# Weaving the last third of a linear attention with the first output tiles, and pairing half-array products, in a one-layer hybrid decoder

## The chip, the cores and the metric

The kernel runs on one core of one Trainium2 chip. Its time is the device time of one execution in microseconds (us). Three runs of the kernel before gave 1269.86, 1271.31 and 1274.69 us, so the median is 1271.31 us. One further execution was profiled; all rows below are from it.

A core has five engines with instruction queues of their own: PE (matrix products; a stationary matrix is loaded first, the loads are counted as PEld), DVE and ACT (vector work), POOL (slower vector work), and SP, which here issues all transfers between the main memory and the core's own memory. Each engine runs its instructions in the order in which they stand in its queue.

## What is computed

One inference step of a single decoder layer for a prompt of 2048 positions and for 8 samples of 8 new positions each (64 rows, called "the sample"; its attention reads a cache of 2048 positions per sample):

```python
h = rmsnorm(x, norm_w)
z = h @ w_in                      # 1024 -> 3600 columns
q, k, v, qb, kb, vb, g_lr, gate_a, gate_b = split(z)
o_a = dilated_attention(rope(rmsnorm(q)), rope(rmsnorm(k)), v)   # (128,1), (512,4), (2048,16)
log_a = log_sigmoid(g_lr @ w_gate_up + b_gate) / 16
o_b, state = gated_linear_attention(qb, kb, vb, log_a, s0)       # exact, in chunks
mixed = concat(o_a * silu(gate_a), rmsnorm(o_b) * silu(gate_b))
y = x + mixed @ w_out
```

The outputs are y for the prompt and the sample, the new keys and values, and the final states of the linear attention.

## The kernel before

**Precision.** The large products run in half precision with each factor split in a high and a low part. A prompt tile of 128 rows needs high·high, high·low and low·high: for each of the 8 slices of 128 along the inner dimension, three products of 128x512 columns, 24 in all (line 1742 for the input projection, line 2088 for the output). For the sample, high and low parts of its 64 rows stand side by side as the 128 columns of one stationary matrix (`hs`, `mh_s`), so that a product with the high weights gives both, and a second product with the low weights gives high·low and, unasked, low·low. That is 16 products for each block of columns (`sample_sum`, line 1434, and `finish` with n = 64). Afterwards the two halves of the 128 result rows are added.

**Stages.** The first stage projects q, k and v tile by tile and runs the first two dilations of the attention behind them (tiles `s`, `p`, `pt`, `t`, `O`). The second projects `qkb`, then `g` and `vb`, with the third dilation beside it. The linear attention of the prompt (`gla_prompt`, eight pieces e0 to e7 of 256 rows, that is 16 chunks; `gla_core` holds seven levels per piece, products `sc_e` at lines 853 and 869; the chunk's state update `U` at line 1900 and output `O` at lines 1908 and 1914) runs beside `g`, `vb` and `gb`. Then the scaled output weights `w_o0` and `w_o1` are made (`load_w`: a maximum over the weights through two small PE products `mx_o`, then eight steps on ACT, line 1272, and on DVE, line 1273). The last stage makes 16 output tiles (`prompt_out`): `combine` joins the three attention branches and the linear attention's output (`oc`, `mix`), `turned` transposes (`tm`, line 2052), `finish` multiplies (`Y`, two column blocks of 24 products) and adds x (`xr`, line 2095). The attention of the sample over its cache (`sample_pair`, products `OS` at line 2344 over value blocks `sv_b` of 1 MB, loaded at line 2375) runs beside it.

**What sets the order.** Two things. The Python code is written as generators, and `weave` takes the next step of the generator with the smallest share done, where each generator has a number of steps written beside it; this sets the order in which buffers of a pool are handed on. From that, `Plan` reads the instructions' dependences, forms priorities, changes some of them by a table of triples (`steps`) and lays down a fixed order for each engine. The table names instructions by number, so any change in the code asks for another table.

**Pools.** In the kernel before, `gla_all` (the linear attention) belongs to the `until` list of the weave with `gb` and the output weights, so in the code it is complete before `prompt_out` begins. The memory of the linear attention's pools (`c_gla`) is then released, and the sample attention's pools (`sk2` with six buffers of 1 MB for `sv_b`, and `ss1`) take its place: the first `sv_b` load cannot start before the last chunk has been stored.

## Time and profile before

| what | value |
|---|---|
| median of 3 runs | 1271.31 us |
| profiled execution | 1268.54 us |
| its span, first to last instruction | 1266.8 us |
| mean granted PE clock | 0.994 |
| PE busy | 1200.7 us, 95% |
| DVE busy | 956.7 us, 76% |
| ACT busy | 816.5 us, 64% |
| POOL busy | 553.5 us, 44% |
| mean rate of the transfers | 223 GB/s |

Times in the rows are counted from the span's first instruction. A row of groups or of the timeline names the line of the kernel, the engine, the operation, output<-inputs (buffer numbers left out), partitions x elements, the count, and in brackets how long the engine stood idle before it and what it waited for. A PE product takes longer from its start to its end than the distance at which products follow each other, so the cost of one is read from start to start. A product of 32-bit factors is two PE instructions in the profile.

### The profile page before, as it was taken

To read this page: it belongs to the slowest core of one execution; us is meant where nothing else is said; L and a number is where in the kernel's file an instruction comes from. 1 tells how busy PE (TensorE), PEld (TensorE's weight loads), DVE (VectorE), ACT (ScalarE), POOL (GpSimd) and SP (SyncE) were. 2 spreads that over 40 slices of the span, in tenths; PEclk is the share of its full clock that TensorE was granted. 3 is DMA by queue.
4 is the path that set the end of the run, shared out by engine and by line. 5 is a ranking of instruction groups with operands and counts; after the bars stand their busy time and mean duration, and the time that the engine had idled before them with its cause. 6 is when DMAs were issued, how large, how long until landed. Compare 5 with 4: busy or idle time off the path is not lost. (4 is left out here: it accounts for less than half of the span.)

```text
span 1266.8 us, 26198 instructions
## 1 busy us (share of the span) xinstructions
PE 1200.7 (95%) x8942; PEld 725.5 (57%) x8942; DVE 956.7 (76%) x2450; ACT 816.5 (64%) x2191; POOL 553.5 (44%) x475
## 2 busy tenths in 40 slices
PE   4999999999999899998999999999999979999998
PEld 2444465666567566766676756656555544545443
DVE  7887787899978867768777764798999793657652
ACT  6654597889589877968677642778779751322230
POOL 0154543666646334542443676655553341323310
PEclk9999999999999999999999999999999999999999
DMA  8579935876866798799999877675647279979941
GB/s 292 183 201 251 258 122 137 227 217 191 205 163 162 202 257 268 229 253 248 253 247 239 252 216 203 175 230 141 236 159 247 80 226 390 384 278 366 351 144 57
DMA packets 235831, 283.07 MB, mean 223 GB/s; under 512 B 116193, under 2 KB 146866, under 8 KB 232626
## 3 DMA queue, kind: packets, MB, share of 16 engines
q1 hardware_dynamic: 235698, 281.40, 74.7%
q8 instruction: 70, 1.15, 0.4%
q14 instruction: 63, 0.52, 0.1%
HBM read 183.02 MB, written 75.24 MB: 204 GB/s over the span
## 5 line engine op out<-in xcount | busy, mean ns | idle before, releaser
L1597 POOL TENSOR_TENSOR pr<-k,qb 128x512 f32<-128x512 f32 x128 | 167.0, 1304 | 178.4 <-DVE sck L1598 109.7
L1742 PEld LDWEIGHTS <-hr 128*128 128x128 f16 x1824 | 172.8, 98 | 114.1 <-issue 12.4
L1033 ACT ACTIVATE p<-p,o 128x256 f32<-128x256 f32 (+1 forms) x384 | 173.1, 456 | 31.5 <-DVE o L1030 29.0
L1742 PEld LDWEIGHTS <-hl 128*128 128x128 f16 x1248 | 119.9, 98 | 122.8 <-issue 10.3
L2088 PE MATMUL Y<-w_o,mh 128*128 128x512 f16 x768 | 178.8, 379 | 5.0 <-DVE w_o L1273 4.1
L1007 POOL TENSOR_TENSOR pt<-p,pt 128x512 f16<-128x512 f32 (+1 forms) x80 | 93.9, 1175 | 121.2 <-ACT pt L1006 112.9
L1055 PE MATMUL O<-v,pt 128*128 128x128 f16 x1200 | 131.4, 220 | 8.9 <-DVE pt L1003 2.5
L1040 PE MATMUL t<-ident,p 128*128 128x128 f32 x600 | 118.8, 279 | 3.3 <-DMA hr<-h_d 1.9
L2088 PEld LDWEIGHTS <-mh 128*128 128x128 f16 x768 | 72.1, 98 | 86.5 <-issue 12.2
L1598 DVE TENSOR_REDUCE sck<-pr 128x8 f32<-128x512 f32 x128 | 87.0, 680 | 43.6 <-POOL pr L1597 43.0
L1055 PEld LDWEIGHTS <-pt 128*128 128x128 f16 x1200 | 93.5, 98 | 39.0 <-POOL pt L1007 5.1
L1742 PE MATMUL acc_v<-w_v,hl 128*128 128x512 f16 x384 | 109.9, 381 | 0.1
L1742 PE MATMUL acc_q<-w_q,hl 128*128 128x512 f16 x384 | 106.4, 383 | 1.1 <-ACT zs_k L1317 0.8
L1742 PE MATMUL acc_k<-w_k,hl 128*128 128x512 f16 x384 | 104.1, 379 | 2.5 <-DVE vp L1404 2.5
L1742 PE MATMUL acc_g<-w_g,hr 128*128 128x272 f16 (+1 forms) x768 | 105.9, 278 | 0.0
L1742 PE MATMUL acc_vb<-w_vb,hr 128*128 128x512 f16 x384 | 97.6, 383 | 1.7 <-DVE so_g L1291 1.6
L1030 DVE CUSTOM_DVE_ANT_0 p<-s,m3w,scl_s 128x128 f32<-128x128 f32 (+1 forms) x256 | 87.8, 394 | 13.4 <-DMA o_d<-o 5.7
L1022 PE MATMUL s<-kk,qq 128*128 128x256 f16 (+1 forms) x512 | 88.2, 266 | 8.6 <-DMA kk<-kp_d 4.8
L1742 PE MATMUL acc_gb<-w_gb,hr 128*128 128x512 f16 x384 | 94.5, 380 | 0.1
L1040 PEld LDWEIGHTS t<-ident,p 128*128 128x128 f32 x600 | 75.0, 142 | 21.5 <-ACT p L1033 8.7
L2130 POOL TENSOR_TENSOR oc<-oc 128x512 f32<-128x512 f32 x32 | 42.4, 1343 | 100.8 <-DVE oc L2123 58.7
L1742 PE MATMUL acc_qkb<-w_qkb,hr 128*128 128x512 f16 x288 | 79.8, 379 | 0.0
(528 smaller groups left out, 2524.3 us busy)
## 6 DMA issues: line engine op xcount, KB each, us to landing
k<-in_cache_k_win SPq DMA_DIRECT2D x104, 256.0 KB
sv_b<-in_cache_v_win SPq DMA_DIRECT2D x24, 1024.0 KB
hr<-h_d SPq DMA_DIRECT2D x44, 512.0 KB
qb<-q_d SPq DMA_DIRECT2D x64, 256.0 KB
oc<-o_d SPq DMA_DIRECT2D x48, 264.0 KB
o_d<-o SPq DMA_DIRECT2D x64, 132.0 KB
x<-in_x_prompt SPq DMA_DIRECT2D x16, 512.0 KB
h_d<-hl SPq DMA_DIRECT2D x16, 512.0 KB
```

The lines of the kernel that those rows point to most:

```text
L1007: POOL.tensor_tensor(l, f, h, ALU.subtract)
L1022: PE.matmul(s_ps[:, i * w : (i + 1) * w], q, k, start=(n == 0), stop=(n == len(prods) - 1),)
L1030: DVE.tensor_tensor_reduce(s[:, sl], s_ps[:, sl], mask, neg, BIG, ALU.add, ALU.min, nmf(i))
L1033: ACT.activation(s[:, sl], s[:, sl], AF.Exp, bias=nmf(i), scale=-1.0, accum_out=denf(i))
L1040: PE.transpose(p_ps[:, i * P : (i + 1) * P], t["s"][:, i * P : (i + 1) * P], ident[:])
L1055: PE.matmul(o_, t["pt"][:, c, (i * nb + b) * P : (i * nb + b + 1) * P], vf(i, b), start=(n == 0), stop=(n == 2 * nb - 1),)
L1597: POOL.tensor_tensor(pr[:], kt, qt, ALU.mult)
L1598: DVE.tensor_reduce(out, pr[:].rearrange("p (u k d) -> p u k d", u=2, k=4), AX.X, ALU.add)
L1742: PE.matmul(z, a_[:, k, :], w[:, p_, k, cols], start=(k == 0 and i == 0), stop=(k == KT - 1 and i == 2),)
L2088: PE.matmul(Y[:], a_[:, k, :], w_[:, part, k, :512], start=(i == 0), stop=(i == len(prods) - 1),)
L2130: eng.tensor_tensor(o_[g], o_[g], w[:, g].unsqueeze(2).to_broadcast([P, NH, HD]), ALU.mult)
```

## The change

Four edits, and a new table.

1. **Half products.** A new function `sample_products` replaces the 16 full products of the sample. The 8 with high weights stay as they were. The 8 with low weights now use only the 64 columns of the high part as the stationary matrix, and put their 64 result rows in turn into the lower and the upper half of the accumulator; the sum of the two halves, which is taken afterwards anyway, holds all of them. The product low·low is no longer computed. This holds for the eight column blocks of the input projection (v, q, k, qkb, g0, g1, vb, gb) and the two of the output.
2. **Weave.** `gla_all` gets 60 instead of 155 steps in the first weave and 10 instead of 45 in the one with `gb`, which makes it take fewer turns there; it leaves the `until` list of that weave, and what is left of it is woven with `prompt_out` (60 steps). `combine(t+2)` waits until its chunk is done.
3. **Scales.** `inv_o0` and `inv_o1` (line 2217) are made before the output tiles begin, in another pool; the tile `bnd` is gone and `smx` serves in its place.
4. **Pools.** The small tiles `qs` and `qr` of the q and k projection move from pool `sm` to pool `xp`.
5. **Plan.** Another table of steps; 3 instead of 12 rounds of priorities, and 800 instead of 900 ns added to a transfer's landing.

```diff
-                ss = sm.tile([P, 2 * NH], F32, name=f"qs_{nm_}_{t}", tag="qs")
+                ss = xp.tile([P, 2 * NH], F32, name=f"qs_{nm_}_{t}", tag="qs", bufs=2)
...
+        def sample_products(out, hs, w, order):
+
+            for i, k in enumerate(order):
+                PE.matmul(out, hs[:, k, :], w(0, k), start=(i == 0), stop=False)
+            for i, k in enumerate(order):
+                r0 = NS * (i % 2)
+                PE.matmul(
+                    out[r0 : r0 + NS], hs[:, k, 0:NS], w(1, k), start=False, stop=(i >= KT - 2)
+                )
+
         def sample_sum(acc, w, hs, c0, ncol):
 
-            prods = [(part, k) for k in range(KT) for part in range(2)]
-            for i, (part, k) in enumerate(prods):
-                PE.matmul(
-                    acc[:, :ncol], hs[:, k, :], w[:, part, k, c0 : c0 + ncol],
-                    start=(i == 0), stop=(i == len(prods) - 1),
-                )
+            sample_products(
+                acc[:, :ncol], hs, lambda part, k: w[:, part, k, c0 : c0 + ncol], range(KT)
+            )
...
-        gla_all = [chain(sample_gla(), *(gla_prompt(e) for e in range(8))), 155]
+        gla_all = [chain(sample_gla(), *(gla_prompt(e) for e in range(8))), 60]
...
-        gla_all[1] = 45
+        gla_all[1] = 10
...
+                if n < P:
+                    sample_products(Y[:], mh, lambda part, k: w_[:, part, k, :512], ks)
+                for i, (k, a_, part) in enumerate(prods if n == P else ()):
...
                     if i == 1 and t + 2 < NT:
+                        while t + 2 not in mixed:
+                            yield WAIT
                         mixes[t + 2] = combine(t + 2)
...
-        weave(host, gla_all, fetch, mixed_first, until=[host, gla_all, fetch, mixed_first])
+        left = weave(host, gla_all, fetch, mixed_first, until=[host, fetch, mixed_first])
+        for nh in range(2):
+            DVE.tensor_scalar(
+                inv_o[nh][:], p2[:], loaded[f"o{nh}"][1][:], 1.0 / M_SCALE, ALU.mult, ALU.mult
+            )
+        out = [prompt_out(), 2 * NT * KT + 30]
+        if left:
+            gla_all = left[0]
+            gla_all[1] = 60
+            out = weave(gla_all, out, until=[gla_all])[0]
...
-        "1:9738:-1587 1:8521:-604 0:11378:-6896 2:12183:-36893 0:12042:-1940 0:7618:-507 "
+        "0:7339:-3039 0:9273:-5212 1:8590:-9900 0:9000:-2297 1:10685:2313 0:13065:3357 2:11182:-7159 "
...
-    plan.fix(plan.settle(12, 900.0, 1.15, 60.0, 10.0, steps))
+    plan.fix(plan.settle(3, 800.0, 1.15, 60.0, 10.0, steps))
```

Line numbers move: what stood at 1742 stands at 1749, 2088 at 2095, 2375 at 2383. The new half products are at line 1440, the full ones of the sample at 1437.

How the order moves, at three places. First PE where the sample's product of block `gb` stands. Before, its 16 full products (line 1438) stand there. Now, in the middle of its low-weight part (`hs` is the sample's stationary matrix, `hr_15` that of prompt tile 15, `sc_e0` a level of the linear attention's first piece, `O_s` the linear attention of the sample):

```order
L1749 MATMUL acc_vb_15_12620<-w_vb_8468,hr_15_11930 128x512
L1440 LDWEIGHTS hs_249
L1440 MATMUL acc_gb_s_12731<-w_gb_11380,hs_249 64x512
L869 MATMUL sc_e0_1_10056<-qbd0_9599,kq_e0_10021 64x64 x8
L1977 MATMUL O_s_9879<-vb_s_9873,Ac_smp_9675 64x128
L1749 LDWEIGHTS hr_15_11930
```

Here a half stands alone among other products; five of the eight halves of this block do. For the other nine blocks the two halves of a pair stand next to each other.

Second PE around the last chunk of the linear attention, `O_15`. Before, within the first output tile:

```order
L2052 MATMUL tm_1_1_14329<-ident16_83,mt_1_14077 128x128
L2088 LDWEIGHTS mh_0_14119
L2088 MATMUL Y_0_0_14217<-w_o0_13586,mh_0_14119 128x512
L1908 MATMUL O_15_13304<-Sbd1_9605,kq_e7_13053 128x256
L1914 MATMUL O_15_13304<-vb_15_13297,full_9609 128x128 x2
```

And now:

```order
L2095 MATMUL Y_4_1_14566<-w_o1_13492,mh_4_14424 128x512
L2095 LDWEIGHTS mh_5_14591
L2095 MATMUL Y_5_0_14642<-w_o0_13018,mh_5_14591 128x512
L1915 MATMUL O_15_14790<-Sbd1_9605,kq_e7_14281 128x256
L1921 MATMUL O_15_14790<-vb_15_14783,full_9609 128x128 x2
```

The last chunk moves from the first output tile to the sixth; chunks 8 to 15 now stand behind the last products of `gb`.

Third the queue of SP where the first value blocks of the sample are loaded. Before:

```order
L914 DMA ob_d_66<-ob_c15_13329 128x512
L2077 DMA xr_3_14675<-in_x_prompt 128x1024
L2105 DMA oc_4_14510<-o1_d_67 128x528
L2105 DMA oc_4_14510<-o2_d_68 128x528
L2105 DMA oc_4_14510<-o3_d_69 128x528
L2260 DMA Sc_0_14280<-sc_d_70 128x2x128
L2302 DMA sm_0_14475<-in_c_smask 128x448
L2304 DMA mc_0_14477<-in_c_smult 128x64
L2375 DMA sv_0_0_b2_14574<-in_cache_v_win 128x2048
```

And now:

```order
L2112 DMA oc_10_15218<-o3_d_69 128x528
L2118 DMA gal_10_15225<-ga_d_65 128x512
L2225 DMA out_state_gla_prompt<-Sbd0_9601 64x128
L2106 DMA out_y_prompt<-xr_4_14492 128x1024
L2118 DMA obl_11_15381<-ob_d_66 128x512
L2118 DMA gwl_11_15382<-gw_d_64 128x512
L914 DMA ob_d_66<-ob_c15_14815 128x512
L2085 DMA xr_8_15209<-in_x_prompt 128x1024
L2268 DMA Sc_0_14924<-sc_d_70 128x2x128
L2310 DMA sm_0_15069<-in_c_smask 128x448
L2383 DMA sv_0_0_b2_15128<-in_cache_v_win 128x2048
```

The first value block stood behind the operands of output tile 4 (`oc_4`); it now stands behind those of tile 10.

## The prediction

> **What bounds the kernel now.** I read the totals first, then PE by stage, then PE's waits in the worst stage.

> ```profile
> PE 1200.7 (95%) x8942; PEld 725.5 (57%) x8942; DVE 956.7 (76%) x2450; ACT 816.5 (64%) x2191; POOL 553.5 (44%) x475
> ```

> PE is busy for 1200.7 of 1266.8 us; 66.1 us are left in which it stands. The table by stage (length, then busy time of PE, PEld, DVE, ACT and POOL, PE's clock, the share and rate of the transfers) says where:

> ```profile
> 0.00:50.00 50.00, 33.07 (x189) 17.41 (x190) 38.14 (x100) 27.10 (x45) 0.85 (x7) 1.00 0.80 274
> 50.00:1000.00 950.00, 916.51 (x6900) 581.02 (x6899) 761.55 (x2007) 715.03 (x2020) 485.21 (x412) 0.99 0.76 209
> 1000.00:1050.00 50.00, 39.89 (x317) 23.71 (x316) 41.96 (x103) 25.57 (x55) 20.06 (x19) 1.00 0.62 206
> 1050.00:1250.00 200.00, 198.77 (x1485) 98.07 (x1484) 110.57 (x236) 48.75 (x73) 47.38 (x38) 1.00 0.79 297
> 1250.00:1266.80 16.80, 12.44 (x58) 5.31 (x56) 4.50 (x6) 0.00 (x0) 0.00 (x0) 0.99 0.15 47
> ```

> PE stands 16.9 us at the start, 33.5 us spread over 950 us, 10.1 us in the 50 us between the linear attention and the output tiles, 1.2 us in the output stage and 4.4 us at the end. So PE's own work sets the time, and the one hole with a place of its own is the third row. What PE waited for in it:

> ```profile
> PE Y L2088 <- DVE w_o L1273: 4.1, 2, 2.1
> PE U L1900 <- DVE Sbd L1921: 1.9, 1, 1.9
> PE tk L2293 <- DVE qx L2256: 1.2, 1, 1.2
> PE tm L2052 <- ACT mh L2053: 1.1, 1, 1.1
> ```

> DVE is late in three of four. In two of its ten-us slices there:

> ```profile
> 1020.00:1030.00 10.00, 8.31 (x53) 4.99 (x54) 9.77 (x25) 6.85 (x15) 5.45 (x4) 1.00 0.70 212
> 1030.00:1040.00 10.00, 4.96 (x29) 2.17 (x29) 9.97 (x15) 4.72 (x11) 4.57 (x4) 1.00 0.86 254
> ```

> DVE is full while PE is half idle: the last chunks, the second output weights and the first output tiles' joining all meet on DVE, whereas in the output stage behind it DVE works 110.6 of 200 us. DVE's rows give the order of events for `w_o1`:

> ```profile
> 1011.66 0.27 DVE L1193 TENSOR_REDUCE mm_o<-mx_o 1x1 f32<-1x128 f32 x1
> 1021.65 0.14 DVE L1184 TENSOR_SCALAR pw_o<-pw_o 128x1 int32<-128x1 int32 x1
> 1025.36 1.58 DVE L1273 SCALAR_TENSOR_TENSOR w_o<-wr_o,ns_o,w_o 128x512 f16<-128x512 f32 x1
> 1033.91 1.76 DVE L1273 SCALAR_TENSOR_TENSOR w_o<-wr_o,ns_o,w_o 128x512 f16<-128x512 f32 x1
> ```

> From the maximum to the last slice of `w_o1` pass 24.0 us (1011.66 to 1035.67), and PE has only the first block of tile 0 and the last chunks to fill them.

> **Term 1, the half products: -4.4 us.** A full product of 512 columns costs 0.216 us on PE, and all of the sample's are on PE's own path:

> ```profile
> 1245.10 6.91 PE Y_s L2088 x32
> 1021.07 0.66 PE L1900 MATMUL U<-vb,kdt_e 128*64 128x128 f32 x8 [1.87 <-DVE Sbd L1921]
> 1021.66 1.25 PE L2088 MATMUL Y<-w_o,mh 128*128 128x512 f16 x5
> 1025.09 0.59 PE L1908 MATMUL O<-Sbd,kq_e 128*128 128x256 f32 x2
> 1025.52 0.61 PE L1914 MATMUL O<-vb,full 128*128 128x128 f32 x4
> 1025.97 0.60 PE L1908 MATMUL O<-Sbd,kq_e 128*128 128x256 f32 x2
> ```

> 32 products in 6.91 us is the 0.216. No half product in 16-bit form is in this trace; the nearest row is `U`, 64 columns wide and alternating between the halves in 32-bit form. Its four products take 0.59 us (1021.07 to the next at 1021.66); two full ones of the same length, `O`, take 0.45 us (1025.52 to 1025.97). So two pairs cost as much as two full products plus 0.14 us for the run: pairs do overlap, and a run of narrow products has a price at its ends. By the order, the 80 half products (64 of 512 columns, 16 of 272 or 256) stand in 20 runs, with 37 pairs, 29 wide and 8 short, and 6 halves without a partner, all in `gb`. Saved: 29 x 0.216 + 8 x 0.11 (0.216 scaled by columns) = 7.2 us; paid: 20 x 0.14 = 2.8 us. I take the `U` row in full, -4.4; bounds: -7.2 if a 16-bit run has no price, +2.8 if pairs do not overlap and the runs cost. Nothing else is added: the accumulator's two halves are read as before.

> The loads of the half matrices speak against it:

> ```profile
> L1900 PEld LDWEIGHTS U<-vb,kdt_e x128: 132/137/138, 816.4 to 1021.3; 128*64 128x64 f32 x128
> L1438 PEld LDWEIGHTS <-hs x128: 95/98/152, 19.7 to 850.4; 128*128 128x128 f16 x128
> ```

> The narrow load takes 137 ns against 98, yet eight of them went into the 0.59 us, so they overlap each other and I charge nothing. [...]

> **Term 2, the hole before the output tiles: -8.0 us.** The half of the linear attention's chunks that stood ahead of the output tiles now stands among the first five. In PE's order, between the maximum of `w_o1` (second `mx_o1`) and its last use in tile 0, stood 24 products of `Y_0_0` and those of `Y_0_1` as they came; now 14 of `gb` and 47 of `Y_0` stand there, 61 x 0.216 = 13.2 us, and besides chunks 8 and 9, each 0.59 us of `U` and twice the 0.88 us of `O` from 1025.09 to 1025.97, 4.7 us together, and 40 products of levels and 32 transposes, which I don't count. So PE has at least 18 us of work while DVE makes `w_o1`, for which it needed 24.0 us; and on DVE seven of its eight slices now stand together, with no chunk update and no joining between. Two of the four waits above lose their cause: `w_o` (4.1), and `Sbd` (1.9), since chunks 14 and 15 no longer follow each other with nothing between. `qx` and `mh` go to places where PE has two blocks `Y` in turn. Cover for each is the output stage, whose DVE had 89 us free. I leave 2.1 of the 10.1 us: bounds -10.1 and 0 (the hole only moves). What is late next: the first evacuation `xr_0`, behind the scales of all tiles; in DVE's order it follows the last `w_o1` slice by 30 instructions, about 11 us by the mean durations of their lines, while PE has 46 products of tile 0 (9.9 us), a chunk and two transposed halves of the next tile.

> **Term 3, the start: -1.5 us.**

> ```profile
> 15.36 0.28 DVE L1193 TENSOR_REDUCE mm_v<-mx_v 1x1 f32<-1x128 f32 x1 [0.33 <-PE mx_v L1191]
> 17.66 0.58 PE L1194 MATMUL mx_v<-mm_v,one_row 1*128 1x1 f32 x2
> 20.87 0.59 PE L1438 MATMUL acc_v_s<-w_v,hs 128*128 128x512 f16 x1 [1.79 <-ACT w_v L1272]
> ```

> The second `mx_v` product stood behind 16 transposes and began 2.0 us after its operand (15.64); in the new order it stands right behind the first small transposes, and on DVE the scale follows it at once. The chain to the first `w_v` slice shortens by that and by a reduction ahead of it, but the eight slices still take ACT and DVE 6 us, so I take -1.5 between 0 and -2.4.

> **Term 4, the sample's values: +1.0 us.** They start later and have less time.

> ```profile
> 1025.97 0.60 PE L1908 MATMUL O<-Sbd,kq_e 128*128 128x256 f32 x2
> 1033.32 0.33 SPq L914 DMA_DIRECT2D ob_d<-ob_c  x1
> 1037.67 0.38 SPq L2260 DMA_DIRECT2D Sc<-sc_d  x1
> 1039.42 2.61 SPq L2375 DMA_DIRECT2D sv_b<-in_cache_v_win  x4
> L2344 PE MATMUL OS<-sv_b,P3x x256: 379/379/403, 1060.1 to 1209.5; 128*32 128x256 f32 x128
> 1050.00:1210.00 160.00, 158.77 (x1264) 78.55 (x1263) 94.66 (x208) 39.93 (x62) 43.56 (x35) 1.00 0.92 347
> ```

> The first block is issued 13.9 us after the last `O` begins (1025.5), because its memory is the linear attention's. Before, PE then had until 1209.5 for the last `OS`. In the new order the first `OS` comes 27 us of PE work behind the last `O`, the last one 117 us behind it. In this stretch SP issues about 35.6 MB; at the 347 GB/s of the last row that takes 103 us, ending 14 + 103 + 2 for landing = 119 us behind. That row's transfers were busy for 0.92, so at full share 377 GB/s and 110 us. It is tight, and behind a late `sv_b` stand the rest of `oc_11` to `oc_13` in SP's queue, for which the joining on DVE waits. I take 1 us; bounds 0 and +19, the latter at the 297 GB/s of 1050 to 1250 (14 + 120 + 2 - 117).

> **The rest: 0.** Every engine's order is new. The 33.5 us between 50 and 1000 have no single cause; the largest waits there:

> ```profile
> PE s L1022 <- DVE o L1030: 4.9, 7, 1.7
> PE s L1022 <- DMA kk<-kp_d: 4.8, 3, 3.3
> ```

> Nothing in the diff removes them, and where the projections end and `qkb` begins the order still leaves PE attention alone. I take 0, and -10 to +12 for the range: a third of it gone, or two more holes like that of 400 to 450 (6.2 us). The moved small tiles and the scales add no instruction that PE waits for.

> Sum: 1268.5 - 4.4 - 8.0 - 1.5 + 1.0 = 1255.6 us beside the profiled execution, which was 2.8 us under the median of the runs (1271.3). For a median I say **1258 us**.

> **The rivals.** *Half products are charged in full* (chance 0.12): pairs do not overlap in 16-bit form, because loads or drains stand between them. For: no such row exists, and the lone halves of `gb` show what that looks like. Against: `U` and `OS` overlap. Price 4.4 + 2.8 = 7.2 us: 1265 us.

> *The hole only moves* (0.10): DVE now has to join tiles and run chunks at once, and what PE loses in 1000 to 1050 it loses again among tiles 0 to 5. For: DVE is at 9.8 of 10 there. Against: its 89 us of room behind. 1266 us.

> *The values of the sample come too late* (0.13), the slower side. The place is the `OS` of the second to fourth pair, tiles 8 to 11. Each load waits for the buffer that `OS` three loads earlier frees, so a stall repeats; SP's queue then delays `oc` and `xr` too. It decides from about 20 us of stall, that is below some 295 GB/s over the stretch (35.6 MB in 117 + 20 - 16 us); 25 us would give 1282 us. For: a mean of only 297 GB/s over the old output stage. Against: that mean holds slices in which little was asked for, and it was 347 while values were loaded.

> *The new plan also closes holes in the middle* (0.13): a third of 33.5 us, 1247 us. For: nothing but the amount that is there.

> **How the numbers follow.** The forecast keeps 0.52, with its own range 1251 to 1265. Half a per cent is 6.4 us, about what a measurement of this kernel can tell from no change: faster is under 1265.0, slower above 1277.7. Faster: 0.50 of the forecast, 0.13 of the last rival and 0.08 of the first two: 0.71. Same: 0.16. Slower: 0.13. The range reaches up to 1274, which takes in the first two rivals, and down to 1246, which takes in the last.

> **What would show it.** In the changed kernel's profile: a run of half products in which the second of a pair starts within 10 ns of the first and 4 pairs take about 1.0 us (right), or 1.7 us (wrong); the mx_o1 to last `w_o1` time under 20 us and PE's idle time in the 50 us around the first `Y` near 2 us; the first `acc_v_s` near 19 us; waits of PE on `sv_b` loads of a few us at most. The forecast is wrong if PE's idle time between 50 and 1000 leaves 33.5 us by more than 10, or if PE stands at `OS` for 10 us and more.

## The result, and the profile after

The changed kernel took 1250.31 us (median of 4 runs, 1250.13 to 1253.41) where the kernel before took 1270.83 (4 runs), a ratio of 0.984 (95% interval 0.981 to 0.986): 20.5 us faster. Two further comparisons, made as the base of the experiments, gave 0.987 (0.984 to 0.990) and 0.989 (0.987 to 0.992), that is 16.6 and 13.8 us. The changed kernel took about the same in all three (1250.3, 1249.8 and 1251.4 us); the kernel before took 1270.8, 1265.5 and 1263.6, and why it differs is open. So the gain is 14 to 20 us. The forecast was 13.3 us under the median (1258 against 1271.3). The profiled execution took 1250.2 us and its span is 1248.1, 18.7 us less than before.

The totals of the changed kernel (busy time, share of the span, instructions):

```profile
PE 1198.9 (96%) x8942; PEld 717.5 (57%) x8942; DVE 955.2 (77%) x2450; ACT 820.2 (66%) x2191; POOL 550.0 (44%) x475
```

The table by stage (length, then busy time of PE, PEld, DVE, ACT and POOL, PE's clock, share and rate of the transfers; the fourth row is a part of the fifth):

```profile
0.00:50.00 50.00, 33.27 (x183) 16.86 (x184) 40.50 (x103) 30.94 (x52) 1.29 (x7) 0.97 0.77 269
50.00:1000.00 950.00, 923.98 (x6852) 574.37 (x6851) 763.68 (x1991) 711.90 (x1990) 482.78 (x410) 1.00 0.77 213
1000.00:1050.00 50.00, 49.87 (x407) 29.18 (x407) 48.29 (x120) 28.86 (x62) 23.64 (x21) 1.00 0.73 241
1050.00:1100.00 50.00, 48.16 (x362) 27.27 (x362) 39.96 (x99) 19.50 (x43) 21.16 (x20) 1.00 0.85 300
1050.00:1230.00 180.00, 178.01 (x1443) 91.50 (x1439) 98.28 (x233) 48.49 (x90) 42.27 (x37) 1.00 0.82 305
1230.00:1248.10 18.10, 13.76 (x70) 5.59 (x68) 4.49 (x6) 0.00 (x0) 0.00 (x0) 0.99 0.14 44
```

PE stands 49.2 us in all, 16.9 less than before, and is busy 1.8 us less. The hole of 10.1 us between 1000 and 1050 is closed to 0.1; in the 50 us behind it PE now stands 1.8 us (0.3 before). But the middle, 50 to 1000, has also gone from 33.5 to 26.0 us, which the prediction had put at nothing. The start is the same (16.9 to 16.7), and so is what follows 1050 (5.6 to 6.3). These are stretches of equal time, not of equal work: `w_o1` now lies ahead of 1000, and chunks 8 to 15 stand further back. Of PE's waits of before, those for `w_o`, `Sbd` and `qx` are gone, and nothing large has come in their place (us in total, times, longest):

```profile
PE mx_v L1191 <- DVE w_v L1248: 14.7, 1, 14.7
PE t L1040 <- ACT p L1033: 3.6, 10, 0.9
PE s L1022 <- DVE o L1030: 3.3, 5, 1.0
...
PE tm L2060 <- DVE Ac_e L875: 1.2, 2, 0.8
...
PE Y L2095 <- DVE xr L2102: 0.6, 1, 0.6
```

In the changed kernel's timeline, the maximum of `w_o1`, its last six slices on DVE, and PE's first products of `Y`:

```profile
966.68 0.27 DVE L1193 TENSOR_REDUCE mm_o<-mx_o 1x1 f32<-1x128 f32 x1
...
981.49 4.05 DVE L1273 SCALAR_TENSOR_TENSOR w_o<-wr_o,ns_o,w_o 128x512 f16<-128x512 f32 x6
...
982.00 0.60 PE L2095 MATMUL Y<-w_o,mh 128*128 128x512 f16 x2
```

From the maximum to the last slice pass 18.9 us (966.68 to 985.54), 24.0 before, and the six last slices stand together. All of it lies ahead of 1000, under the work on `gb` and the chunks.

The half products, in PE's timeline: a run of eight in the last tile, and lone halves in `gb`:

```profile
812.61 0.40 PE L1440 MATMUL acc_gb_s<-w_gb,hs 128*64 128x512 f16 x1
812.95 0.39 PE L1749 MATMUL acc_vb<-w_vb,hr 128*128 128x512 f16 x1
813.27 0.40 PE L1440 MATMUL acc_gb_s<-w_gb,hs 128*64 128x512 f16 x1
813.60 0.39 PE L1749 MATMUL acc_vb<-w_vb,hr 128*128 128x512 f16 x1
...
1229.55 0.81 PE L1437 MATMUL Y_s<-w_o,mh_s 128*128 128x512 f16 x3
1230.29 1.05 PE L1440 MATMUL Y_s<-w_o,mh_s 128*64 128x512 f16 x8
1231.28 0.60 PE L1437 MATMUL Y_s<-w_o,mh_s 128*128 128x512 f16 x2
```

Eight halves take 0.99 us from their first start to the next product (1230.29 to 1231.28), where eight full ones take 1.73: pairs overlap. But the three full products ahead of them take 0.74 us (1229.55 to 1230.29) instead of 3 x 0.216 = 0.65. And a lone half with the full product behind it takes 0.66 us (812.61 to 813.27) instead of 0.43: the full one, which stands ahead of the next half, takes 0.32. So a run of halves costs 0.09 us ahead of its first start and 0.13 behind that, 0.22 us together, not 0.14.

### The profile page after: what moved, and what is told of

Its sections match the earlier page's. It is cut to its first block, busy times and chain, and to the rows that moved or that the text cites. A ratio compares the mean times of both kernels' runs of the same rounds, so it can differ in the third digit from the quotient of the medians.

```text
span 1248.1 us, 26183 instructions
## 1 busy us (share of the span) xinstructions
PE 1198.9 (96%) x8942; PEld 717.5 (57%) x8942; DVE 955.2 (77%) x2450; ACT 820.2 (66%) x2191; POOL 550.0 (44%) x475
## 4 chain that ended last, share of the span: by engine, by line
PE 61%; DVE 17%; ACT 10%; DMA 5%; issue 4%; POOL 2%; SPq 1%; POOLq 0%; DVEq 0%; ACTq 0%
PE Y L2095 9%; PE acc_q L1749 5%; PE acc_v L1749 5%; PE acc_vb L1749 4%; PE acc_k L1749 4%; PE t L1040 4%; PE acc_qkb L1749 4%; PE acc_g L1749 4%; PE O L1055 4%; PE s L1022 4%; PE acc_gb L1749 2%; PE OS L2352 2%; ACT p L1033 1%; DVE p L1030 1%; DMA qb<-q_d 1%
## 5 line engine op out<-in xcount | busy, mean ns | idle before, releaser
L1033 ACT ACTIVATE p<-p,o 128x256 f32<-128x256 f32 (+1 forms) x384 | 173.1, 456 | 22.9 <-DVE o L1030 20.2
L2095 PE MATMUL Y<-w_o,mh 128*128 128x512 f16 x768 | 181.8, 379 | 1.1 <-DVE xr L2102 0.6
L1055 PE MATMUL O<-v,pt 128*128 128x128 f16 x1200 | 134.6, 219 | 4.1 <-ACT pt L1002 1.9
L1749 PE MATMUL acc_k<-w_k,hl 128*128 128x512 f16 x384 | 108.9, 379 | 1.4 <-DVE vp L1404 1.4
L1749 PE MATMUL acc_q<-w_q,hl 128*128 128x512 f16 x384 | 109.2, 379 | 0.0
L1030 DVE CUSTOM_DVE_ANT_0 p<-s,m3w,scl_s 128x128 f32<-128x128 f32 (+1 forms) x256 | 86.9, 395 | 8.7 <-PE s L1022 2.2
L1040 PEld LDWEIGHTS t<-ident,p 128*128 128x128 f32 x600 | 73.8, 141 | 27.8 <-ACT p L1033 13.8
L1022 PE MATMUL s<-kk,qq 128*128 128x256 f16 (+1 forms) x512 | 84.6, 264 | 5.4 <-DVE o L1030 3.3
```

Of the source, the lines that this page charges most:

```text
L1022: PE.matmul(s_ps[:, i * w : (i + 1) * w], q, k, start=(n == 0), stop=(n == len(prods) - 1),)
L1030: DVE.tensor_tensor_reduce(s[:, sl], s_ps[:, sl], mask, neg, BIG, ALU.add, ALU.min, nmf(i))
L1033: ACT.activation(s[:, sl], s[:, sl], AF.Exp, bias=nmf(i), scale=-1.0, accum_out=denf(i))
L1040: PE.transpose(p_ps[:, i * P : (i + 1) * P], t["s"][:, i * P : (i + 1) * P], ident[:])
L1055: PE.matmul(o_, t["pt"][:, c, (i * nb + b) * P : (i * nb + b + 1) * P], vf(i, b), start=(n == 0), stop=(n == 2 * nb - 1),)
L1749: PE.matmul(z, a_[:, k, :], w[:, p_, k, cols], start=(k == 0 and i == 0), stop=(k == KT - 1 and i == 2),)
```

## The experiments

Where an order is called fixed, the order of all five engines was written out as a list of the 13290 instructions, so that nothing but the edit differs from the changed kernel. Differences in us are differences of the two ratios to the kernel before, times its median in that comparison (1263.6 to 1266.1); the interval of a ratio is about 0.25% to either side, 3 us, so a difference of two ratios is known to some 4 us. The times at which PE reaches a product are from one execution of each kernel.

**The base.**

> The changed kernel once more, as the base for the others of this group: 1250.3 us by every theory.

Measured: 1249.78 us, ratio 0.9869 (0.9843 to 0.9895).

**Full products in the new order** (order fixed; the low weights' products compute low·low again).

```diff
-                r0 = NS * (i % 2)
-                PE.matmul(
-                    out[r0 : r0 + NS], hs[:, k, 0:NS], w(1, k), start=False, stop=(i >= KT - 2)
-                )
+                PE.matmul(out, hs[:, k, :], w(1, k), start=False, stop=(i == KT - 1))
```

> The changed kernel with the low weights' products of the sample full again (128 columns of the stationary matrix, whole accumulator), each at the place in PE's order where the half product stood; the order of all engines is held fixed. Term 1 of the prediction (a run of halves costs 0.14 us): 4.4 us slower than the changed kernel, 1254.7. The changed kernel's trace, where the product ahead of a run takes 0.31 us to the next start instead of 0.216, the first pair 0.24 and the last half 0.31: 0.22 us for a run, 20 runs, so 7.2 - 4.4 = 2.8 us slower, 1253.1. Rival, the time that PE gains there goes into its next wait: 1250.3 within 1 us.

Measured: 0.9883 (0.9860 to 0.9907), 1.8 us slower than the base by the ratios, 2.9 by the medians. That is on the side of 2.8 rather than 4.4, but the intervals overlap. Alone it settles neither the size nor whether there is a gain at all: the rival's zero lies within the interval too.

**Neighbours in the same half** (order fixed).

```diff
-                r0 = NS * (i % 2)
+                r0 = NS * (i // 4)
                 PE.matmul(
-                    out[r0 : r0 + NS], hs[:, k, 0:NS], w(1, k), start=False, stop=(i >= KT - 2)
+                    out[r0 : r0 + NS], hs[:, k, 0:NS], w(1, k), start=False, stop=(i % 4 == 3)
                 )
```

> The changed kernel, same order of all engines, with the eight half products of a block in another choice of half: the first four all in the lower, the last four all in the upper half of the accumulator, so that neighbours share a half. If pairs overlap only because they lie in different halves: 24 more slots of 0.212 us and 6 of 0.106 on PE, 5.7 us slower than the changed kernel, 1256.0. If narrow products overlap whatever half they take, or if their loads set the pace: 1250.3.

Measured: 0.9888 (0.9865 to 0.9912), 2.4 us slower than the base, between the two. The timeline says why. Four halves of `k`, in the changed kernel:

```profile
185.05 0.62 PE L1440 MATMUL acc_k_s<-w_k,hs 128*64 128x512 f16 x4
185.60 0.73 PE L1055 MATMUL O<-v,pt 128*128 128x128 f16 x10
```

and in this one, with a run of eight behind it:

```profile
184.52 1.05 PE L1440 MATMUL acc_k_s<-w_k,hs 128*64 128x512 f16 x4
185.50 0.73 PE L1055 MATMUL O<-v,pt 128*128 128x128 f16 x10
...
1234.09 1.06 PE L1440 MATMUL Y_s<-w_o,mh_s 128*64 128x512 f16 x8
1235.09 0.39 PE L1437 MATMUL Y_s<-w_o,mh_s 128*128 128x512 f16 x1
```

Four halves that all go to one half of the accumulator take 0.98 us instead of 0.55, one after another. Eight, the first four below and the last four above, take 1.00 us, as little as alternating ones. So in these runs two products overlap where they lie in different halves, as assumed, but they need not be neighbours. The last four, which alone would take 0.98 us as well, add 0.02 us to the first four, so the fifth must have started beside the first. With that, only runs that hold unequal numbers for the two halves lose: by the run lengths (four runs of 2, two of 4, one of 6, one of 2, one of 3) 11 slots of 0.212 us, 2.3 us. That fits the 2.4 measured, though these times alone do not separate it from zero.

**Runs of two** (order fixed).

```diff
-            for i, k in enumerate(order):
-                PE.matmul(out, hs[:, k, :], w(0, k), start=(i == 0), stop=False)
+            for j in range(0, KT, 2):
+                for k in order[j : j + 2]:
+                    PE.matmul(out, hs[:, k, :], w(0, k), start=(k == order[0]), stop=False)
+                for i, k in enumerate(order[j : j + 2]):
+                    PE.matmul(
+                        out[NS * i : NS * i + NS], hs[:, k, 0:NS], w(1, k),
+                        start=False, stop=(j == KT - 2),
+                    )
```

> The changed kernel, same places in all orders, but in a block two full products take turns with two halves instead of eight full ones ahead of eight halves: 50 runs of halves instead of 20, and 8 pairs fewer (1.7 us). At 0.14 us for a run (the prediction's price, from the U row): 4.2 + 1.7 = 5.9 us slower than the changed kernel, 1256.2. At 0.22 us (the changed kernel's trace): 6.6 + 1.7 = 8.3 us, 1258.6. If a change of width costs nothing: 1252.0.

Measured: 1259.21 us, 0.9940 (0.9917 to 0.9962), 9.0 us slower than the base. That a change of width costs something is clear of the noise; the size is nearer to 0.22 us for a run (8.3 expected) than to 0.14 (5.9), but the two are closer than the 4 us. The timeline decides. Its last tile, two full ones and two halves in turn:

```profile
1239.41 0.41 PE L1440 MATMUL Y_s<-w_o,mh_s 128*64 128x512 f16 x2
1239.74 0.60 PE L1438 MATMUL Y_s<-w_o,mh_s 128*128 128x512 f16 x2
1240.28 0.41 PE L1440 MATMUL Y_s<-w_o,mh_s 128*64 128x512 f16 x2
```

The period is 0.87 us, and four full products take 0.86: a run of one pair earns nothing at all.

**Whole runs** (the changed kernel's orders; on PE the eight halves of a block moved to where the last of them stood).

> The changed kernel, same order on all engines but PE; on PE the eight halves of each block stand together, where the last of them stood: 10 runs instead of 20, 40 pairs instead of 37. At 0.22 us for a run: 2.2 + 0.6 = 2.8 us faster than the changed kernel. At 0.14 us: 2.0 us faster. If the halves that stood between other products filled time in which PE waited anyway: no difference.

Measured: 1249.49 us, 0.9872 (0.9850 to 0.9895), against 0.9891 (0.9867 to 0.9916) for the changed kernel in the same comparison (1251.37 us):

> The changed kernel once more, as the base for the others of this group: 0.985 to 0.987 of the kernel before.

2.4 us faster, between the 2.8 at 0.22 us a run and the 2.0 at 0.14; the intervals overlap, so the best version found here is faster by an amount that these runs do not separate from zero.

**The tables and the weave.** Three kernels without a table, ordered by the planner alone:

```diff
-        "0:7339:-3039 0:9273:-5212 ...
+    steps = ""
```

and in the third also

```diff
-        gla_all = [chain(sample_gla(), *(gla_prompt(e) for e in range(8))), 60]
+        gla_all = [chain(sample_gla(), *(gla_prompt(e) for e in range(8))), 155]
...
-        gla_all[1] = 10
+        gla_all[1] = 45
...
-        left = weave(host, gla_all, fetch, mixed_first, until=[host, fetch, mixed_first])
+        left = weave(host, gla_all, fetch, mixed_first, until=[host, gla_all, fetch, mixed_first])
```

> The kernel before with an empty table (the planner's own order, 12 rounds and 900 ns as before). It says what the old table is worth. No row bears on it; if the tables are worth the same, it loses as much against the kernel before as the kernel without the new table loses against the changed one.

> The changed kernel with an empty table. If the code (halves 2.8 us, weave 8 us, start 1.5 us) carries the gain, as the prediction's terms 1 to 3 say, it is 12 us faster than the kernel before without its table (e5). If the gain is the table's, the two are equal.

> As e6, but the linear attention gets its old steps (155, then 45) and ends in the weave ahead of the output tiles, as before; halves, scales, pools and planner's numbers stay. Term 2 of the prediction: 8 us slower than e6, with PE idle for 8 to 10 us in the 50 us around the first Y. Rival, the hole only moves or the weave needs its table: equal to e6 within 2 us.

Measured, against the kernel before: 1.0166 (1.0136 to 1.0196), 1.0073 (1.0044 to 1.0102) and 1.0205 (1.0177 to 1.0232). So without any table the changed code, with its planner's numbers (3 rounds and 800 ns against 12 and 900), is worth 11.8 us (12 expected), and the old weave costs 16.7 us (8 expected). That the 12 came out as a sum looks like luck: the third kernel, which has all of the code's change but the weave, is 4.9 us slower than the first, where halves and start were to make it 4.3 us faster. With an uncertainty of about 5 us, that shows no gain from halves, pools, scales and planner's numbers, and it does not tell them apart. The old table is worth 21 us to the kernel before, the new one 23 to 26 us to the changed kernel, by its two later ratios. Around the first `Y`, with the new weave:

```profile
1000.00:1050.00 50.00, 48.01 (x373) 27.70 (x371) 46.71 (x102) 28.51 (x63) 25.19 (x21) 0.98 0.65 222
1050.00:1100.00 50.00, 48.09 (x327) 27.81 (x327) 46.59 (x122) 22.02 (x55) 22.35 (x20) 0.98 0.70 237
```

and with the old one:

```profile
1000.00:1050.00 50.00, 44.57 (x292) 25.07 (x291) 37.35 (x82) 27.16 (x59) 15.45 (x16) 0.97 0.42 149
1050.00:1100.00 50.00, 43.25 (x398) 21.25 (x396) 23.73 (x53) 11.21 (x21) 10.69 (x9) 0.90 0.91 347
```

PE stands 12.2 us in these 100 us instead of 3.9, and that is the 8 of Term 2. The kernel before, without its table, stands 11.6 us there. On top, its clock is 0.97 and 0.90 instead of 0.98 twice: 13 in 100 of 50 us lost instead of 4 in 100, 4.5 us more. The last 4 us are elsewhere and were not followed.

**The order of the first half.** In both kernels the first 7460 instructions of the code are the same but for the halves (the projections v, q, k, qkb and most of the attention). Their relative order on all engines was exchanged between the two kernels, the rest kept.

> The changed kernel; the instructions up to the end of the projection qkb and the attention written ahead of it in the code (the first 7460, the same in both kernels but for the halves) follow each other on every engine as in the kernel before, the rest as in the changed kernel. If the new plan closed holes in the first 570 us (the changed kernel starts acc_g_s 4.5 us earlier, of which halves and their runs give about 1.5): 3 us slower than the changed kernel. The prediction's zero for the rest: no difference. If that half holds all of the extra gain: 7 us slower.

> The kernel before, full products and old weave, with the same first 7460 instructions in the changed kernel's order on every engine and the rest in its own: the reverse of h1. Plan closes holes there: 3 us faster than the kernel before, by the markers. The prediction's zero: no difference, or 1.5 us faster by Term 3 alone, which lies in this half.

As whole runs both took 1296.07 us (1.0252, 1.0229 to 1.0275) and 1306.02 us (1.0326, 1.0304 to 1.0349), 32 and 41 us slower than the kernel before, and slower still against the changed one. By the traces the loss comes behind the seam, where the two orders no longer fit each other. The worst 100 us of the first and of the second:

```profile
900.00:1000.00 100.00, 83.25 (x614) 47.11 (x610) 82.24 (x198) 66.42 (x158) 44.59 (x44) 0.93 0.55 187
```

```profile
700.00:800.00 100.00, 82.44 (x522) 51.75 (x520) 45.17 (x135) 43.52 (x131) 54.45 (x53) 0.86 0.64 174
```

PE stands there for 17 us each time. Neither theory spoke of that, so their times say nothing on it. What can still be read is the time at which PE reaches the first product behind the exchanged part, `acc_g_s`; this reading was chosen after the runs. Before, and in the changed kernel:

```profile
569.85 0.28 PE L1438 MATMUL acc_g_s<-w_g,hs 128*128 128x272 f16 x1
```

```profile
565.38 0.40 PE L1437 MATMUL acc_g_s<-w_g,hs 128*128 128x272 f16 x2
```

The changed kernel with the old first half, and the kernel before with the new one:

```profile
572.41 0.28 PE L1437 MATMUL acc_g_s<-w_g,hs 128*128 128x272 f16 x1
```

```profile
564.72 0.40 PE L1438 MATMUL acc_g_s<-w_g,hs 128*128 128x272 f16 x2
```

With the old order PE gets there at 569.9 and 572.4, with the new one at 564.7 and 565.4, whether the products are full or half. So the 4.5 us that the changed kernel is ahead at this point go with the order, and the halves of v, q, k and qkb show no gain that stands out there. Each is one execution; six others with the new order, one of them with full products, reached it at 562.7 to 566.2, and the runs of two at 569.6. What made the order is shown by the kernels without a table. The changed code, without its table:

```profile
571.69 0.28 PE L1437 MATMUL acc_g_s<-w_g,hs 128*128 128x272 f16 x1
```

With the old weave it is 572.9, and the kernel before without its table is there at 571.3. So neither the halves nor the weave, the pools or the planner's numbers bring the lead at this point: it is the new table's.

**Fewer buffers for the sample's values** (order fixed).

```diff
-                    pool, tag, bufs = (zp, ("z3", "z4")[bb], 1) if n == 1 else (ssk, "sv4", 6)
+                    pool, tag, bufs = (zp, ("z3", "z4")[bb], 1) if n == 1 else (ssk, "sv4", 4)
```

> The changed kernel, same order of all engines, with four instead of six buffers of 1 MB for the sample's values sv_b, so that every load from the fifth on waits for an OS one step earlier than now (12 steps of two loads stand between 1099 and 1190 us, 7.5 us each). If the stream is as tight as Term 4 says (119 us needed where 117 are there): a step's 2 MB take 5.5 us at 361 GB/s and 2 to land, all of the 7.5 us, so PE stands about 1 us at each of ten steps, 10 us slower than the changed kernel. If there is room (in the changed kernel's trace the first loads are issued 20 us ahead of their OS, and PE waits 0.4 us for sv_b in all): within 2 us of the changed kernel.

Measured: 1258.84 us, 0.9952 (0.9934 to 0.9969), 7.7 to 10.5 us slower than the changed kernel by its two later ratios. The larger products `OS` and the loads in the changed kernel:

```profile
L2352 PE MATMUL OS<-sv_b,P3x x256: 379/379/403, 1101.1 to 1189.6; 128*32 128x256 f32 x128
...
L2383 SPq DMA_DIRECT2D sv_b<-in_cache_v_win x24: 328/333/689, 1078.7 to 1169.6; - x24
```

and with four buffers:

```profile
L2352 PE MATMUL OS<-sv_b,P3x x256: 379/379/634, 1100.3 to 1198.7; 128*32 128x256 f32 x128
```

From the first to the last of them pass 98.4 us instead of 88.5. But PE did not lose a little at each step. It waited twice for a transfer:

```profile
1105.44 1.06 PE L2352 MATMUL OS<-sv_b,P3x 128*32 128x256 f32 x2 [3.26 <-DMA sv_b<-in_cache_v_win]
...
1135.71 1.03 PE L2301 MATMUL tk<-ident,k 128*128 128x128 f32 x4 [1.79 <-DMA k<-in_cache_k_win]
```

The first wait, by single us, and what follows it:

```profile
1102.00:1103.00 1.00, 0.18 (x4) 0.00 (x0) 0.00 (x0) 0.00 (x0) 0.00 (x0) 1.00 0.75 270
...
1105.00:1106.00 1.00, 0.56 (x2) 0.18 (x2) 0.00 (x0) 0.00 (x0) 0.00 (x0) 0.56 0.99 418
1106.00:1107.00 1.00, 1.00 (x5) 0.29 (x4) 0.00 (x0) 0.18 (x1) 0.00 (x0) 0.50 1.03 428
1107.00:1108.00 1.00, 1.00 (x5) 0.46 (x4) 0.00 (x0) 0.85 (x1) 0.00 (x0) 0.50 1.01 328
1108.00:1109.00 1.00, 1.00 (x5) 0.47 (x4) 0.00 (x0) 0.00 (x0) 0.40 (x1) 0.73 1.07 404
```

PE stands for 3.3 us, and then its clock is at half for about as long: 0.44 + 0.50 + 0.50 + 0.27 = 1.7 us more. The second wait, 1.8 us for a key block whose load stood in SP's queue behind two value blocks (issued at 1127.8 and 1128.6), is followed by the same 1.7 us (a clock of 0.73 and 0.84 in the two stretches of 4 us from 1134 on). With a third of 1.1 us for `xr` this makes 9.6 of the 9.9 us.

Does that show the stream of Term 4 to be tight? No. The first three steps of `OS` follow each other closely (1099.4, 1101.1 and 1106.2 in the changed kernel), and with four buffers the blocks of the third can only be asked for when the first is done. That is a shortage of buffers at one place, not of rate over the stretch.

## Why the prediction was right, and where it was wrong

The direction, the range and the main mechanism held: the result lies between the forecast and the rival that closes holes in the middle, and that rival came true beside the forecast, not in its place. That 1258 less the rival's 7.5 us gives just what was measured is luck in part: Terms 1 and 3 gave 1.6 and 1.5 us less than forecast, a faster clock's 3.9 us stood in no term, and 4.9 us are not accounted for (see below).

*Term 1, the half products (-4.4).* The mechanism was right: pairs overlap, and 4 pairs take 0.99 us though their loads are narrow. The 137 ns of the narrow load were no sign against that: they are a 32-bit load, and loads of full width in 32 bits take 141 ns (line 1040) to 191 ns (line 1908) in the same profile. The halves' 16-bit loads take 110 ns against 98. No run shows the drains of the first rival as such, only a price for each run. The size was off. The step that failed is the price of a run, 0.14 us from the `U` row, which was read from the first start of the run to the next product; the 0.09 us ahead of the first start are in the product before it, and no row of the run itself shows them. At 0.22 us the 20 runs cost 4.4 us of the 7.2, and the term is -2.8. The runs of two agree with 0.22 by their timeline and lie nearer to it by their total; the whole runs fit both prices. No run separates the 2.8 us themselves from zero: with full products in the same order the kernel was 1.8 us slower, give or take 4.

*Term 2, the hole before the output tiles (-8.0).* Right: 10.1 to 0.1 in its 50 us, and 10.4 to 2.0, that is 8.4 us, with the 50 us behind. The named signs came out, 18.9 us for `w_o1` where under 20 was forecast, 0.1 us of standing where about 2 was. That the weave does this without a table was shown by taking it back without a table: 8.3 us more of standing there. The term has no price for the clock. In the kernel before it needed none, since the clock was 1.00 in that hole; without a table the old weave lost 4.5 us by it.

*Term 3, the start (-1.5).* The sign named for it came: the first `acc_v_s` begins at 18.87 (20.87 before). The gain did not. In the changed kernel's timeline:

```profile
18.87 0.61 PE L1437 MATMUL acc_v_s<-w_v,hs 128*128 128x512 f16 x1
...
27.77 1.05 PE L1440 MATMUL acc_v_s<-w_v,hs 128*64 128x512 f16 x8
28.75 0.45 PE L1126 MATMUL th<-ident,early_ht 128*128 128x128 f16 x5
```

and before:

```profile
28.32 0.38 PE L1438 MATMUL acc_v_s<-w_v,hs 128*128 128x512 f16 x1
```

The block ends where it ended. The eight slices of the weights that ACT and DVE make set its pace, and with the full products first all eight must be there before the first half product. The prediction named these slices as the reason to take less than the bound, but still took 1.5; the bound 0 was the value, and PE's standing in the first 50 us fell by 0.2 only.

*Term 4, the sample's values (+1.0).* No wait of PE for `sv_b` is in the list of the changed kernel, so the bound 0 was the value, and "tight" was wrong. The first block is issued at 1078.7, 7.5 us behind the start of the last `O` (1071.2) and not 14, and the last at 1169.6, 98 us behind it, where the term has 119 for its landing. The last step of `OS` begins 18.5 us after that issue. The 2 us for landing were an estimate and fit: of the two blocks issued at 1123.7 and 1124.1 in the changed kernel the first had landed 4.7 us after its issue and the second 2.5 us behind it, so that 2.2 of the 4.7 us are not the transfer of its 1 MB. Of the nine pairs of loads behind the first six blocks, six are issued just as the `OS` that used their buffers ends, so buffers set their pace and not the rate; no run tested the rate itself.

*The rest (0).* This is the step that was wrong by most. PE stands 7.5 us less between 50 and 1000. The reason given for zero was that nothing in the diff removes those waits; but the diff holds a new table, and a table is what places such waits: without it the lead at `acc_g_s` is gone. Up to that product PE stands 5.0 us less from 50 us on (20.2 to 15.2). The kernel before with the new order of the first half stands 13.5 us there; the changed kernel with the old order stands 16.2, so that most of its 7 us of delay lie inside PE's busy time. Where the other 2.5 us come from was not tested. The rival for this had 0.13 and a price of a third of the 33.5 us, 11; it was 7.5.

*What does not add up.* PE's standing fell by 16.9 us and its slowed clock by 3.9 (a clock of 0.994 over 1266.8 us loses 7.6, one of 0.997 over 1248.1 loses 3.7). With 2.8 for the halves that is 23.6 us, and the span fell by 18.7. The 4.9 us between lie inside PE's busy time, which hides short waits: a product of 512 columns is listed with 0.38 us where the next starts 0.22 us behind it. No run here took them apart.

## What to carry to other kernels

The price of changing the width of PE's products is read from the start of the product ahead of the narrow run, not from the run's first start. Here it was 0.22 us a run and a pair saved 0.216, so that halves of 512 columns in 16-bit form pay only in runs of four and more, with equal numbers for each half. And where a table or a planner's numbers are part of a change, the waits that it may move belong in the sum with both signs, even if no edit names them: here that zero hid 7.5 us of standing.

## What the runs showed of the hardware that was not expected

**Some waits of PE were paid twice.** Behind some holes PE's clock is at half for 3.4 us, so that such a hole costs up to 1.7 us more than its length. The kernel before has four such places in its profile, slow from 187.8, 351.7, 580.4 and 686.2 on; two of them by windows of 4 us:

```profile
346.00:350.00 4.00, 1.30 (x9) 0.55 (x7) 2.37 (x3) 0.38 (x1) 3.68 (x3) 1.00 0.97 204
350.00:354.00 4.00, 3.43 (x15) 1.83 (x15) 2.17 (x9) 2.58 (x9) 0.00 (x0) 0.71 1.07 271
...
576.00:580.00 4.00, 2.36 (x33) 1.90 (x31) 2.58 (x11) 3.92 (x13) 1.68 (x2) 1.00 1.18 212
580.00:584.00 4.00, 3.55 (x15) 2.00 (x15) 3.57 (x6) 4.00 (x8) 0.75 (x1) 0.57 0.89 186
```

PE stands 2.7 and 1.6 us in the first row of each pair, at full clock, and is slow in the second. The changed kernel has two such places, slow from 46.1 and 834.6 on. Most holes are not charged: of the 15 waits of 1 us and more between 50 and 1050 in the kernel before, three are followed by a slow clock, and the three of 1.9 to 2.1 us in the hole ahead of the output tiles are not. A wait of 1.8 us near 832 is charged in one profile of the changed kernel and not in another.

**Each half of the accumulator took its own products.** Without pairs of neighbours, four products of one half took 0.98 us, one after another; the run of eight with the first four below and the last four above took 1.00 us, and the run of six (four below, two above, in `qkb`) 0.99 us (425.83 to 426.82). So the fifth must have run beside the first although three others stood between them in PE's queue: the order of that queue, which an engine was said to keep, was kept in these two runs within each half, and not between the halves.
